# The last norm of a two-layer transformer kernel: squares summed by products with ones, the root from ACT, the row spread into two banks

## The chip, the cores and the metric

The kernel runs on one core of a Trainium2 chip. The metric is the device time of one execution in microseconds (us); lower is better. Engines are named as the profile names them: PE (TensorE), PEld (its weight loads), DVE (VectorE), ACT (ScalarE), POOL (GpSimd), SP (SyncE, here a DMA queue).

## The reference

A hybrid of two layers over 512 positions and 1024 channels, all in float32. Layer 0 mixes with two kinds of attention, layer 1 with a third; each is followed by a convolution-gated FFN with 2816 hidden channels. At the end the whole residual stream goes through one more norm. What matters here is that last norm and the FFN ahead of it:

```python
def rmsnorm(x, g):
    xf = x.astype(jnp.float32)
    y = xf * lax.rsqrt(jnp.mean(xf * xf, axis=-1, keepdims=True) + EPS) * g.astype(jnp.float32)
    return y.astype(x.dtype)

for layer in range(DEPTH):
    h = rmsnorm(x, attn_norm[layer])
    ...
    x = x + conv_glu_ffn(rmsnorm(x, ffn_norm[layer]), w_up[layer], conv_w[layer], conv_b[layer], w_down[layer])
return rmsnorm(x, final_norm)
```

## The kernel before

The residual stream is held transposed: `xT` has eight tiles of 128 channels by 512 positions. Every product of the network is split into three (`mm3`: high by high, high by low, low by high part), which is why PE has almost 6000 matmuls.

In the second layer's FFN, `ffn(1, fin_tile, fin_half, ...)`, the last group of hidden channels is not added over all 512 columns at once but in two halves of 256, `Q[0]` and `Q[1]`. The first half runs over the tiles d = 0 to 7, the second over 6, 7, 4, 5, 2, 3, 0, 1. For each tile PE makes twelve products of 256 columns (`mm_d`, in one of three banks), and DVE adds them to `xT` (L464). Then `fin_tile` is called: ACT squares the tile (`sq`, L776), DVE adds the square to the sum `acc` (L777), and ACT writes tile times gain to an output buffer `yo`, which holds two tiles. After each half `fin_half` is called. It calls `rstd_of`:

- PE transposes `acc` in two blocks of 128 columns into the bank `st_n` (L187), so that positions lie on partitions, and DVE sums each over its 128 elements (L189): `ms_n`, 128x2.
- DVE scales and adds EPS, makes a first guess of the inverse root from the bits of the number (L191, L192), and refines it three times in three steps each (`h`, `h`, `y`; L194 to L196).
- PE transposes `y`, repeated 128 times, back into a bank `bc_n` (L199): each partition then holds the row of inverse roots.

Then ACT copies `bc_n` to `rb` (L786), because POOL cannot read the banks, and eight multiplications follow: six on DVE straight from the bank, those of tiles 3 and 7 on POOL from `rb` (L789). DVE's first one waits until ACT has read the bank. Four DMAs of two tiles each (256 KB) write the half out, two from SP's queue and two from ACT's (L791).

The order of instructions on each engine is set by a scheduler when the program is built, and it interleaves the first half's norm with the second half's products. Up to the last group of the FFN the two programs have the same order on every engine, apart from one memset.

Of the kernel before, what the change touches and what calls it, by code (L numbers as in the profile page):

```python
# [33 lines left out]
EPS = 1e-6  # L34
# [37 lines left out]
def hybrid_kernel(ctx: ExitStack, tc: tile.TileContext, xT_d, pos_d, const_d, vec_d, w_d, out_d, idx):  # L72
    nc = tc.nc
    V, A, G, PE = nc.vector, nc.scalar, nc.gpsimd, nc.tensor

    cp = ctx.enter_context(tc.tile_pool(name="cp", bufs=1))
    wp = ctx.enter_context(tc.tile_pool(name="wp", bufs=3))
    ap_ = ctx.enter_context(tc.tile_pool(name="ap", bufs=1))
# [9 lines left out]
    def tmp(name):  # L88
        return tp.tile([P, T], F32, tag="tmp", name=name, bufs=N_TMP)

    def col(name, n=1):
        return tp.tile([P, n], F32, tag=f"col{n}", name=name, bufs=N_COL)

    def ps(tag, name, shape=(P, T)):
        return pp.tile(list(shape), F32, tag=tag, name=name, bufs=N_PSUM[tag])
# [3 lines left out]
    vec = cp.tile([P, V_END], F32, name="vec")  # L99
    pos = cp.tile([P, NB], I32, name="pos")  # L100
    xT = cp.tile([P, KT, T], F32, name="xT")
# [5 lines left out]
    V.memset(table, 0.0)  # L107
    A.copy(table, table)
    ident = const[:, C_ID:C_ID + P]
    cmask = cp.tile([P, T], F32, name="cmask")  # L110
    G.memset(cmask[:, :384], 0.0)
    selr = cp.tile([P, P + 8], F32R, name="selr")
# [45 lines left out]
    def proj(name, w=None):  # L158
        wh, wl = w or chunk(name)
        o = ps("mm", f"mm_{name}")  # L160
        for k in range(KT):
            s = slice(k * P, k * P + P)
            mm3(o, wh[:, s], wl[:, s], xh[:, k], xl[:, k], k == 0, k == KT - 1)
        return o
# [18 lines left out]
    def rstd_of(acc, n, nm, nb=NB):  # L183

        st = ps("T", f"st_{nm}")[:, :nb * P]
        for b in range(nb):
            PE.transpose(st[:, b * P:b * P + P], acc[:, b * P:b * P + P], ident)  # L187
        ms, y, h, t = (col(f"{c}_{nm}", nb) for c in ("ms", "y", "h", "t"))
        V.reduce_sum(ms, st.rearrange("p (b c) -> p b c", b=nb), axis=mybir.AxisListType.X)  # L189
        V.tensor_scalar(ms, ms, 1.0 / n, EPS, op0=OP.mult, op1=OP.add)  # L190
        V.tensor_scalar(t.bitcast(I32), ms.bitcast(I32), 1, None, op0=OP.logical_shift_right)  # L191
        V.tensor_scalar(y.bitcast(I32), t.bitcast(I32), -1, 0x5F3759DF, op0=OP.mult, op1=OP.add)  # L192
        for _ in range(3):
            V.scalar_tensor_tensor(h, y, -0.5, y, op0=OP.mult, op1=OP.mult)  # L194
            V.tensor_tensor(h, h, ms, op=OP.mult)
            V.scalar_tensor_tensor(y, h, 1.5, y, op0=OP.add, op1=OP.mult)  # L196
        bc = ps("T", f"bc_{nm}")[:, :nb * P]
        for b in range(nb):
            PE.transpose(bc[:, b * P:b * P + P], y[:, b:b + 1].to_broadcast([P, P]), ident)  # L199
        return y, bc  # L200

    scale = {}
# [23 lines left out]
    def scaled(o, nm):  # L226
        y = tmp(f"sc_{nm}")
        V.tensor_tensor(y, o, RB, op=OP.mult)
        return y
# [37 lines left out]
    def rope_angles():  # L267

        def fl(t):
            return t.rearrange("p b f -> p (b f)")  # L270

        def ang_tile(nm, k=1):
            return cp.tile([P, k * NB, 8], F32, name=f"ang_{nm}")

        def rnd(nm, src, k, c=1):
            t = ang_tile(nm, c)
            V.tensor_scalar(fl(t), fl(src), k, MAGIC, op0=OP.mult, op1=OP.add)
            V.tensor_scalar(fl(t), fl(t), -MAGIC, None, op0=OP.add)
# [12 lines left out]
        r, t = ang_tile("r"), ang_tile("t")
        fma(r, hi, -65536.0, ang)
        n0 = rnd("n0", r, 1.0 / TWO_PI)
        n2 = rnd("n2", hi, BIG / TWO_PI)
        V.tensor_scalar(fl(t), fl(hi), M2[0], None, op0=OP.mult)
        for a, k, dst in ((n0, -PI2[0], r), (n2, -PI2[0], t), (n0, -PI2[1], r), (hi, M2[1], t), (n0, -PI2[2], r),
                          (n2, -PI2[1], t), (hi, M2[2], t), (n2, -PI2[2], t)):
            fma(dst, a, k, dst)
        cs = ang_tile("cs", 2)
        V.tensor_tensor(fl(cs[:, NB:]), fl(r), fl(t), op=OP.add)  # L300
        V.tensor_scalar(fl(cs[:, :NB]), fl(cs[:, NB:]), math.pi / 2, None, op0=OP.add)
        k = rnd("k", cs, 1.0 / TWO_PI, 2)
        for p in PI2:
            fma(cs, k, -p, cs)
        V.tensor_scalar(fl(cs), fl(cs), -math.pi, math.pi, op0=OP.max, op1=OP.min)
        A.activation(fl(cs), fl(cs), AF.Sin)
        return cs
# [245 lines left out]
    def sq_acc(n):  # L553
        return cp.tile([P, T], F32, tag="acc", name=f"acc{n}", bufs=1)


    acc = sq_acc(0)
# [6 lines left out]
    cs = rope_angles()  # L564
# [5 lines left out]
    for d in range(KT):  # L570
        if d < 4:
            square(d, acc)
        else:
            s = acc2 if d == 4 else tmp(f"sq{d}")
# [54 lines left out]
    y = scaled(proj("ckv"), "ckv")  # L629
    sq = tmp("sqkv")  # L630
    A.activation(sq, y, AF.Square)
    _, bc = rstd_of(sq, P, "kv")
# [75 lines left out]
    for n in range(8):  # L708
        c, w = (fox if n < 4 else dsa)(n % 4)
# [13 lines left out]
    acc = sq_acc(1)  # L723
# [18 lines left out]
    def moba(p):  # L742
        def vals():
            values["m", p // 2] = v_group(f"mv{p // 2}_", moba_scale if p == 0 else None)

        def qs():
            c["q"] = stack_q(rope(proj(f"mq{p}"), f"mq{p}"), f"mq{p}")

        def ks():
            c["k"] = stack_k(rope(proj(f"mk{p}"), f"mk{p}"), f"mk{p}")  # L750

        c = {"nm": f"m{p}", "v": ("m", p // 2), "hv": 2 * (p % 2), "bias": causal, "out": mo[p // 4]}
        return c, ([vals] if p % 2 == 0 else []) + [ks, qs]

    pairs, work = [], []
    for n in range(8):
        c, w = moba(n)
# [8 lines left out]
    fin = {}  # L766

    def fin_tile(d, cs):
        if cs.start not in fin:
            fin[cs.start] = True  # L770
            fin["acc"] = sq_acc(4 + cs.start)[:, :256]
            fin["y"] = [None] * 4
            A.activation(fin["acc"], xT[:, d, cs], AF.Square)
        else:
            s = tmp(f"sq{d}")[:, :256]
            A.activation(s, xT[:, d, cs], AF.Square)  # L776
            V.tensor_tensor(fin["acc"], fin["acc"], s, op=OP.add)  # L777
        if fin["y"][d // 2] is None:
            fin["y"][d // 2] = ap_.tile([P, 2, 256], F32, tag="big", name=f"yo{cs.start}_{d}", bufs=N_BIG)
        A.activation(fin["y"][d // 2][:, d % 2], xT[:, d, cs], AF.Identity, scale=vec[:, V_G + 32 + d:V_G + 33 + d])  # L780

    def fin_half(cs):
        y = fin["y"]
        _, bc = rstd_of(fin["acc"], D, f"n4_{cs.start}", 2)
        r = tmp(f"rb{cs.start}")[:, :256]
        A.copy(r, bc)  # L786
        for d in range(KT):
            yd = y[d // 2][:, d % 2]
            (G if d % 4 == 3 else V).tensor_tensor(yd, yd, r if d % 4 == 3 else bc, op=OP.mult)  # L789
        for d in range(0, KT, 2):  # L790
            (nc.sync if d % 4 == 0 else nc.scalar).dma_start(out_d[cs.start // 256, :, d:d + 2], y[d // 2])  # L791
# [110 lines left out]
```

## Time and profile before

| | |
|---|---|
| time, median of 3 runs (range) | 1266.65 us (1266.18 to 1268.14) |
| time of the profiled execution | 1267.01 us |
| span of its profile | 1265.2 us |
| mean granted TensorE clock | 0.993 |
| PE busy | 1221.0 us |
| DVE busy | 814.5 us |
| ACT busy | 555.2 us |
| POOL busy | 359.6 us |
| moved by DMA | 127.24 MB |

The span runs from the first to the last instruction of the profiled execution; the time of an execution holds some 1.8 us more. In timeline rows the columns are start, duration, engine, line, operation, output<-inputs, shape and count, and in brackets how long the engine sat idle before and what ended that wait. A DMA row of a queue (SPq, ACTq) is the issue, not the transfer.

### The profile page before, as it was taken

To read this page: it belongs to the slowest core of one execution; us is meant where nothing else is said; L and a number is where in the kernel's file an instruction comes from. 1 tells how busy PE (TensorE), PEld (TensorE's weight loads), DVE (VectorE), ACT (ScalarE), POOL (GpSimd) and SP (SyncE) were. 2 spreads that over 40 slices of the span, in tenths; PEclk is the share of its full clock that TensorE was granted. 3 is DMA by queue.
4 is the path that set the end of the run, shared out by engine and by line. 5 is a ranking of instruction groups with operands and counts; after the bars stand their busy time and mean duration, and the time that the engine had idled before them with its cause. 6 is when DMAs were issued, how large, how long until landed. Compare 5 with 4: busy or idle time off the path is not lost.

```text
span 1265.2 us, 16798 instructions
## 1 busy us (share of the span) xinstructions
PE 1221.0 (97%) x5980; PEld 1017.5 (80%) x5980; DVE 814.5 (64%) x1512; ACT 555.2 (44%) x966; POOL 359.6 (28%) x394
## 2 busy tenths in 40 slices
PE   6889999999999999999998999999999999999996
PEld 4778877777888888888887888888878888888885
DVE  7889988675555445555665778787655555544556
ACT  5564677554333332333434556556433333333234
POOL 3675556542111111111213323232212111111110
PEclk9999999999999999999999999999999999999998
DMA  5344435222333333323334434431323333333321
GB/s 193 101 113 110 114 95 138 68 82 75 94 108 94 98 101 100 95 90 97 103 100 125 112 101 117 108 106 67 97 87 100 100 101 93 92 98 101 100 84 67
DMA packets 57379, 127.24 MB, mean 101 GB/s; under 512 B 7584, under 2 KB 21024, under 8 KB 57296
## 3 DMA queue, kind: packets, MB, share of 16 engines
q1 hardware_dynamic: 56368, 124.81, 33.6%
q10 hardware_dynamic: 864, 1.17, 0.3%
q8 instruction: 47, 0.77, 0.3%
q14 instruction: 36, 0.29, 0.1%
q0 software_dynamic: 64, 0.20, 0.0%
HBM read 104.13 MB, written 2.10 MB: 84 GB/s over the span
## 4 chain that ended last, share of the span: by engine, by line
PE 79%; DVE 12%; ACT 3%; issue 3%; POOL 2%; DMA 2%; DVEq 0%; ACTq 0%; POOLq 0%; SPq 0%
PE mm_d L155 6%; PE mm_d L156 6%; PE mm_d L154 6%; PE mm_u L155 6%; PE mm_u L154 6%; PE mm_u L156 6%; PE mm_g L155 6%; PE mm_g L156 6%; PE mm_g L154 6%; DVE tmask L625 2%; DVE m L624 1%; PE t_m L367 1%; PE o_m L376 1%; PE mm_mk L154 1%; PE mm_mk L155 1%
## 5 line engine op out<-in xcount | busy, mean ns | idle before, releaser
L429 POOL TENSOR_TENSOR cv<-cv,gs 128x512 f32<-128x512 f32 x44 | 57.1, 1298 | 549.7 <-ACT gs L428 549.7
L154 PE MATMUL mm_d<-a_h,wh_d 128*128 128x512 f32 (+1 forms) x384 | 142.9, 372 | 2.2 <-ACT a_h L126 2.2
L155 PE MATMUL mm_d<-a_l,wh_d 128*128 128x512 f32 (+1 forms) x384 | 142.9, 372 | 0.5 <-DVE a_l L127 0.5
L156 PE MATMUL mm_d<-a_h,wl_d 128*128 128x512 f32 (+1 forms) x384 | 142.6, 371 | 0.0
L498 DVE TENSOR_TENSOR us<-mm_u,cv 128x512 f32<-128x512 f32 x44 | 30.4, 691 | 168.2 <-PE mm_u L156 132.7
L155 PE MATMUL mm_g<-xl,wh_g 128*128 128x512 f32 x352 | 137.2, 390 | 0.4 <-DVE xl L170 0.4
L154 PE MATMUL mm_u<-xh,wh_u 128*128 128x512 f32 x352 | 137.3, 390 | 0.0
L156 PE MATMUL mm_u<-xh,wl_u 128*128 128x512 f32 x352 | 137.0, 389 | 0.0
L155 PE MATMUL mm_u<-xl,wh_u 128*128 128x512 f32 x352 | 137.0, 389 | 0.0
L156 PE MATMUL mm_g<-xh,wl_g 128*128 128x512 f32 x352 | 136.9, 389 | 0.0
L154 PE MATMUL mm_g<-xh,wh_g 128*128 128x512 f32 x352 | 136.9, 389 | 0.0
L143 ACT CAST wh_g<-raw_g 128x1024 fp32r<-128x1024 f32 x44 | 46.3, 1053 | 155.4 <-PE mm_g L155 153.9
L495 DVE TENSOR_TENSOR gs<-mm_g,RB 128x512 f32<-128x512 f32 x44 | 30.4, 690 | 121.8 <-PE mm_g L156 119.4
L126 ACT CAST wh_d<-raw_d 128x1024 fp32r<-128x1024 f32 x45 | 47.4, 1054 | 119.3 <-PE mm_u L155 107.3
L154 PEld LDWEIGHTS mm_d<-a_h,wh_d 128*128 128x128 f32 x384 | 72.3, 188 | 15.5 <-ACT a_h L126 3.0
L155 PEld LDWEIGHTS mm_d<-a_l,wh_d 128*128 128x128 f32 x384 | 72.3, 188 | 13.5 <-DVE a_l L127 1.1
L156 PEld LDWEIGHTS mm_d<-a_h,wl_d 128*128 128x128 f32 x384 | 72.3, 188 | 12.4
L155 PEld LDWEIGHTS mm_g<-xl,wh_g 128*128 128x128 f32 x352 | 66.1, 188 | 14.8 <-DVE xl L170 1.1
L154 PEld LDWEIGHTS mm_g<-xh,wh_g 128*128 128x128 f32 x352 | 66.1, 188 | 13.8
L156 PEld LDWEIGHTS mm_u<-xh,wl_u 128*128 128x128 f32 x352 | 66.1, 188 | 13.7
L155 PEld LDWEIGHTS mm_u<-xl,wh_u 128*128 128x128 f32 x352 | 66.1, 188 | 13.6
L154 PEld LDWEIGHTS mm_u<-xh,wh_u 128*128 128x128 f32 x352 | 66.1, 188 | 13.6
(762 smaller groups left out, 3071.9 us busy)
## 6 DMA issues: line engine op xcount, KB each, us to landing
raw_g<-in_w SPq DMA_DIRECT2D x44, 512.0 KB, 3.5
raw_u<-in_w SPq DMA_DIRECT2D x44, 512.0 KB, 3.6
raw_d<-in_w SPq DMA_DIRECT2D x41, 256.0 KB, 2.9
raw_d<-in_w SPq DMA_DIRECT2D x29, 192.0 KB, 2.6
raw_d<-in_w SPq DMA_DIRECT2D x34, 128.0 KB, 2.4
raw_oe<-in_w SPq DMA_DIRECT2D x8, 512.0 KB, 4.2
raw_mv<-in_w SPq DMA_DIRECT2D x8, 512.0 KB, 3.5
raw_mk<-in_w SPq DMA_DIRECT2D x8, 512.0 KB, 4.0
```

The lines of the kernel that those rows point to most:

```text
L126: A.copy(dst_h, src)
L143: A.copy(wh, raw)
L154: PE.matmul(out, ah, bh, start=first, stop=False)
L155: PE.matmul(out, ah, bl, start=False, stop=False)
L156: PE.matmul(out, al, bh, start=False, stop=last)
L367: PE.transpose(t[:, n * P:n * P + P], probs[i][:, j * P:j * P + P], ident)
L376: PE.matmul(o[:, o0:o0 + w], vj, ph[:, c0:c0 + w], start=j == 0, stop=False)
L429: G.tensor_tensor(cv, cv, gs, op=OP.mult)
L495: V.tensor_tensor(gs, og, RB, op=OP.mult)
L498: V.tensor_tensor(us, ou, cv, op=OP.mult)
L624: V.max(m8, sc)
L625: V.match_replace(sc, m8, sc, -3e38)
```

## The change

The helper `rstd_of` stays for the other norms. For the last one `fin_half` now does the work itself:

- The squares are summed over the partitions by products with a tile of ones (`ones`, 128x2, set at the start): the weights are a block of 128 columns of `acc`, and the moving operand is `ones`. The square of the last tile is no longer added to `acc`; it is summed by a product of its own into the same place. Four products per half replace two transposes, the reduction and one addition. Each sum comes out twice, so the column tiles have four columns.
- The inverse root is the reciprocal by DVE, its square root by ACT, and one refinement in three steps.
- The row is spread twice, into `bc` in one bank (read by DVE) and into `bp` in another (read by ACT for POOL's copy).
- DVE multiplies two tiles at a time (three multiplications of 512 elements), and POOL multiplies both tiles of the last pair, 6 and 7.
- Each DMA is issued after its pair, the pairs 0 and 2 from SP, 1 and 3 from ACT. The buffers' names carry the first tile of the pair, so yo_6 is the last pair.

```diff
+    ones = cp.tile([P, 2], F32, name="ones")
+    V.memset(ones, 1.0)
...
     def fin_tile(d, cs):
...
+        f["sq"] = tmp(f"sq{d}")[:, :256] if f["n"] else f["acc"]
+        A.activation(f["sq"], xT[:, d, cs], AF.Square)
+        if 0 < f["n"] < KT - 1:
+            V.tensor_tensor(f["acc"], f["acc"], f["sq"], op=OP.add)
...
     def fin_half(cs):
-        y = fin["y"]
-        _, bc = rstd_of(fin["acc"], D, f"n4_{cs.start}", 2)
+        f = fin[cs.start]
+        nm = f"n4_{cs.start}"
+        st = ps("T", f"st_{nm}")
+        for b in range(2):
+            s = slice(b * P, b * P + P)
+            PE.matmul(st[:, 2 * b:2 * b + 2], f["acc"][:, s], ones, start=True, stop=False)
+            PE.matmul(st[:, 2 * b:2 * b + 2], f["sq"][:, s], ones, start=False, stop=True)
+        ms, y, h = (col(f"{c}_{nm}", 4) for c in ("ms", "y", "h"))
+        V.tensor_scalar(ms, st[:, :4], 1.0 / D, EPS, op0=OP.mult, op1=OP.add)
+        V.reciprocal(h, ms)
+        A.activation(y, h, AF.Sqrt)
+        V.scalar_tensor_tensor(h, y, -0.5, y, op0=OP.mult, op1=OP.mult)
+        V.tensor_tensor(h, h, ms, op=OP.mult)
+        V.scalar_tensor_tensor(y, h, 1.5, y, op0=OP.add, op1=OP.mult)
+        bc, bp = ps("T", f"bc_{nm}")[:, :256], ps("O", f"bp_{nm}")[:, :256]
+        for o in (bc, bp):
+            for b in range(2):
+                PE.transpose(o[:, b * P:b * P + P], y[:, 2 * b:2 * b + 1].to_broadcast([P, P]), ident)
         r = tmp(f"rb{cs.start}")[:, :256]
-        A.copy(r, bc)
-        for d in range(KT):
-            yd = y[d // 2][:, d % 2]
-            (G if d % 4 == 3 else V).tensor_tensor(yd, yd, r if d % 4 == 3 else bc, op=OP.mult)
-        for d in range(0, KT, 2):
-            (nc.sync if d % 4 == 0 else nc.scalar).dma_start(out_d[cs.start // 256, :, d:d + 2], y[d // 2])
+        A.copy(r, bp)
+        for d, yd in sorted(f["y"].items()):
+            if d == 3:
+                for e in range(2):
+                    G.tensor_tensor(yd[:, e], yd[:, e], r, op=OP.mult)
+            else:
+                V.tensor_tensor(yd, yd, bc.rearrange("p (o c) -> p o c", o=1).to_broadcast([P, 2, 256]), op=OP.mult)
+            (nc.sync if d % 2 == 0 else nc.scalar).dma_start(out_d[cs.start // 256, :, 2 * d:2 * d + 2], yd)
```

Line numbers shift by two, and inside `mm3` L154 to L156 become L156 to L158. The numbers in the names below only count tiles; mm_d_6 is the product for tile 6.

PE, before, where the norm of the first half stands among the second half's first products (mm_d_6 and mm_d_7 are the products of tiles 6 and 7, st_n the bank of the transposed sum):

```order
L154 MATMUL mm_d_6_10963<-a_h,wh_d_18_6_10885 128x256
L155 MATMUL mm_d_6_10963<-a_l,wh_d_18_6_10885 128x256
L156 MATMUL mm_d_6_10963<-a_h,wl_d_18_6_10886 128x256
L187 MATMUL st_n_0_10926<-const,acc_10770 128x128 x2
L154 MATMUL mm_d_7_10981<-a_h,wh_d_18_6_10885 128x256
L155 MATMUL mm_d_7_10981<-a_l,wh_d_18_6_10885 128x256
L156 MATMUL mm_d_7_10981<-a_h,wl_d_18_6_10886 128x256
```

After, at the same place, from the last product of the first half's tile 7 on (`ones`, `acc` and `sq` as in the code):

```order
L158 MATMUL mm_d_7_10910<-a_h,wl_d_18_6_10888 128x256
L790 MATMUL st_n_0_10927<-ones,acc_10772 128x2
L156 MATMUL mm_d_6_10958<-a_h,wh_d_18_6_10887 128x256
...
L158 MATMUL mm_d_6_10958<-a_h,wl_d_18_6_10888 128x256
L791 MATMUL st_n_0_10927<-ones,sq_10924 128x2
L790 MATMUL st_n_0_10927<-ones,acc_10772 128x2
L791 MATMUL st_n_0_10927<-ones,sq_10924 128x2
L156 MATMUL mm_d_6_10958<-a_h,wh_d_18_6_10887 128x256
```

One product now stands straight behind the first half's last product; the other three come nine products later, behind the square of tile 7, where before the two transposes came after all twelve products of tile 6.

PE, before, where the row of the first half is spread (bc_n, bp_n its banks; mm_d_2, mm_d_4 and mm_d_5 the products of tiles 2, 4, 5):

```order
L156 MATMUL mm_d_5_11018<-a_h,wl_d_18_4_10842 128x256
L154 MATMUL mm_d_2_11036<-a_h,wh_d_18_2_10796 128x256
L199 MATMUL bc_n_0_10946<-const,y_n_0_10930 128x128 x2
L155 MATMUL mm_d_2_11036<-a_l,wh_d_18_2_10796 128x256
L156 MATMUL mm_d_2_11036<-a_h,wl_d_18_2_10797 128x256
```

After:

```order
L157 MATMUL mm_d_4_10994<-a_l,wh_d_18_4_10843 128x256
L158 MATMUL mm_d_4_10994<-a_h,wl_d_18_4_10844 128x256
L802 MATMUL bc_n_0_10941<-const,y_n_0_10933 128x128 x2
L802 MATMUL bp_n_0_10942<-const,y_n_0_10933 128x128 x2
L156 MATMUL mm_d_4_10994<-a_h,wh_d_18_4_10843 128x256
```

The spreading moved ahead: it stood behind the first product of tile 2, 25 products after the last one of tile 7, and now stands nine products after it, with twice as many transposes.

DVE, before, in the refinement of the first half's root (wl_d is the low part of the last weight buffer, xT with mm_d the addition of a tile):

```order
L195 TENSOR_TENSOR h_n_0_10931<-h_n_0_10931,ms_n_0_10929 128x2
L196 SCALAR_TENSOR_TENSOR y_n_0_10930<-h_n_0_10931,y_n_0_10930 128x2
L127 TENSOR_TENSOR wl_d_18_0_11078<-raw_d_18_0_11073,wh_d_18_0_11077 128x1024
L194 SCALAR_TENSOR_TENSOR h_n_0_10931<-y_n_0_10930 128x2
L464 TENSOR_TENSOR xT<-xT,mm_d_4_10999 128x256
L195 TENSOR_TENSOR h_n_0_10931<-h_n_0_10931,ms_n_0_10929 128x2
L196 SCALAR_TENSOR_TENSOR y_n_0_10930<-h_n_0_10931,y_n_0_10930 128x2
L464 TENSOR_TENSOR xT<-xT,mm_d_5_11018 128x256
L789 TENSOR_TENSOR yo_0_10772<-yo_0_10772,bc_n_0_10946 128x256 x2
L789 TENSOR_TENSOR yo_2_10817<-yo_2_10817,bc_n_0_10946 128x256
```

After, from the first half's ms_n on:

```order
L793 TENSOR_SCALAR ms_n_0_10932<-st_n_0_10927 128x4
L794 RECIPROCAL h_n_0_10934<-ms_n_0_10932 128x4
L466 TENSOR_TENSOR xT<-xT,mm_d_6_10958 128x256
L466 TENSOR_TENSOR xT<-xT,mm_d_7_10976 128x256
L796 SCALAR_TENSOR_TENSOR h_n_0_10934<-y_n_0_10933 128x4
L797 TENSOR_TENSOR h_n_0_10934<-h_n_0_10934,ms_n_0_10932 128x4
L798 SCALAR_TENSOR_TENSOR y_n_0_10933<-h_n_0_10934,y_n_0_10933 128x4
L810 TENSOR_TENSOR yo_0_10774<-yo_0_10774,bc_n_0_10941 128x512
L810 TENSOR_TENSOR yo_2_10819<-yo_2_10819,bc_n_0_10941 128x512
L810 TENSOR_TENSOR yo_4_10864<-yo_4_10864,bc_n_0_10941 128x512
L777 TENSOR_TENSOR acc_10972<-acc_10972,sq_10990 128x256
L466 TENSOR_TENSOR xT<-xT,mm_d_4_10994 128x256
```

The chain is shorter, its step behind ACT's root now stands after the additions of tiles 6 and 7, and the multiplications of yo stand ahead of the addition of tile 4 and of wl_d.

ACT, before, at the very end (squares and yo of tiles 0 and 1, the copy, two output DMAs):

```order
L776 ACTIVATE sq_11095<-xT 128x256
L780 ACTIVATE yo_0_11098<-xT,vec 128x256
L776 ACTIVATE sq_11114<-xT 128x256
L780 ACTIVATE yo_0_11098<-xT,vec 128x256
L786 COPY rb_11141<-bc_n_256_11138 128x256
L791 DMA out<-yo_2_11053 128x512
L791 DMA out<-yo_6_10979 128x512
```

After:

```order
L775 ACTIVATE sq_11090<-xT 128x256
L781 ACTIVATE yo_0_11093<-xT,vec 128x256
L775 ACTIVATE sq_11109<-xT 128x256
L781 ACTIVATE yo_0_11093<-xT,vec 128x256
L795 ACTIVATE y_n_256_11118<-h_n_256_11119 128x4
L804 COPY rb_11132<-bp_n_256_11127 128x256
L811 DMA out<-yo_6_10974 128x512
L811 DMA out<-yo_2_11048 128x512
```

The root stands ahead of the copy, and the two DMAs have changed places: the one of the last pair (yo_6) is first.

More of the change, by code (lines that the diff above doesn't have):

```diff
@@ L768, in fin_tile @@
     def fin_tile(d, cs):
[L769 to L779, printed above, removed]
@@ L780, in fin_tile @@
-        A.activation(fin["y"][d // 2][:, d % 2], xT[:, d, cs], AF.Identity, scale=vec[:, V_G + 32 + d:V_G + 33 + d])
-    def fin_half(cs):
-        y = fin["y"]
-        _, bc = rstd_of(fin["acc"], D, f"n4_{cs.start}", 2)
-        r = tmp(f"rb{cs.start}")[:, :256]
-        A.copy(r, bc)
-        for d in range(KT):
-            yd = y[d // 2][:, d % 2]
-            (G if d % 4 == 3 else V).tensor_tensor(yd, yd, r if d % 4 == 3 else bc, op=OP.mult)
-        for d in range(0, KT, 2):
-            (nc.sync if d % 4 == 0 else nc.scalar).dma_start(out_d[cs.start // 256, :, d:d + 2], y[d // 2])
+        f = fin.setdefault(cs.start, {"n": 0, "y": {}})
@@ new lines, in fin_tile @@
+        if not f["n"]:
+            f["acc"] = sq_acc(4 + cs.start)[:, :256]
+        f["sq"] = tmp(f"sq{d}")[:, :256] if f["n"] else f["acc"]
+        A.activation(f["sq"], xT[:, d, cs], AF.Square)
+        if 0 < f["n"] < KT - 1:
+            V.tensor_tensor(f["acc"], f["acc"], f["sq"], op=OP.add)
+        f["n"] += 1
+        if d // 2 not in f["y"]:
+            f["y"][d // 2] = ap_.tile([P, 2, 256], F32, tag="big", name=f"yo{cs.start}_{d}", bufs=N_BIG)
+        A.activation(f["y"][d // 2][:, d % 2], xT[:, d, cs], AF.Identity, scale=vec[:, V_G + 32 + d:V_G + 33 + d])
```

## The prediction

> **What bounds the kernel now.** I read the page's first part, then the chain of waits, then the timeline of the last 40 us engine by engine, then the busy time of short windows at the very end.
>
> ```profile
> span 1265.2 us, 16798 instructions
> PE 1221.0 (97%) x5980; PEld 1017.5 (80%) x5980; DVE 814.5 (64%) x1512; ACT 555.2 (44%) x966; POOL 359.6 (28%) x394
> ```
>
> PE is busy for 97% of the span, so nothing off PE matters except where PE has run out of work. That is only after the last down product: the chain that ended last leaves PE there and walks through the final norm of the second half of the columns.
>
> ```profile
> 1252.82 0.13 PE mm_d L156
> 1252.98 0.43 DVE xT L464
> 1253.49 0.42 ACT sq L776
> 1253.94 0.43 DVE acc L777
> ...
> 1254.51 0.42 PE st_n L187 x2
> 1254.96 0.43 DVE ms_n L189
> 1255.41 0.18 DVE ms_n L190
> 1255.62 0.18 DVE t_n L191
> ...
> 1257.59 0.17 DVE y_n L196
> 1257.76 0.14 issue
> 1257.90 0.68 PE bc_n L199 x2
> 1258.65 0.38 ACT rb L786
> 1259.06 0.42 DVE yo L789
> ```
>
> From the end of the last square (1253.49 + 0.42 = 1253.91) to the first multiplication of the output (1259.06) it takes 5.15 us, and none of it lies beside PE work. Behind it stands the output.
>
> ```profile
> 1259.06 2.07 DVE L789 TENSOR_TENSOR yo<-yo,bc_n 128x256 f32<-128x256 f32 x6 [1.30 <-ACT rb L786]
> 1259.10 1.41 POOL L789 TENSOR_TENSOR yo<-yo,rb 128x256 f32<-128x256 f32 x2 [9.81 <-ACT rb L786]
> 1259.83 0.33 SPq L791 DMA_DIRECT2D out<-yo  x1
> 1260.22 0.34 ACTq L791 DMA_DIRECT2D out<-yo  x1
> 1261.21 0.34 ACTq L791 DMA_DIRECT2D out<-yo  x1
> 1260.00:1261.00 1.00, 0.00 (x0) 0.00 (x0) 1.00 (x4) 0.00 (x0) 0.51 (x1) 0.50 0.32 121
> 1261.00:1262.00 1.00, 0.00 (x0) 0.00 (x0) 0.13 (x1) 0.00 (x0) 0.00 (x0) 0.50 1.02 385
> 1263.00:1264.00 1.00, 0.00 (x0) 0.00 (x0) 0.00 (x0) 0.00 (x0) 0.00 (x0) 0.50 0.45 168
> ```
>
> In the window rows the last two columns are the DMA share and GB/s. A share of 0.32 in the slice from 1260 means that data began to move near 1260.68, 0.85 after the first issue at 1259.83; from there the engines are full until 1263.45. So the four pieces of 256 KB take 2.77 us together, 0.69 each, and they end 4.39 us after the first multiplication began.
>
> The same norm of the first half lies inside the PE stream, and costs PE only what its own few products and waits cost:
>
> ```profile
> 1239.88 0.43 DVE L777 TENSOR_TENSOR acc<-acc,sq 128x256 f32<-128x256 f32 x1 [0.55 <-ACT sq L776]
> 1240.15 0.28 PE L154 MATMUL mm_d<-a_h,wh_d 128*128 128x256 f32 x1
> 1241.47 0.28 PE L156 MATMUL mm_d<-a_h,wl_d 128*128 128x256 f32 x1
> 1241.89 0.41 PE L187 MATMUL st_n<-const,acc 128*128 128x128 f32 x2
> 1242.26 0.28 PE L155 MATMUL mm_d<-a_l,wh_d 128*128 128x256 f32 x1
> 1246.45 0.28 PE L154 MATMUL mm_d<-a_h,wh_d 128*128 128x256 f32 x1
> 1246.91 0.40 PE L199 MATMUL bc_n<-const,y_n 128*128 128x128 f32 x2 [0.18 <-DVE y_n L196]
> 1247.27 0.28 PE L156 MATMUL mm_d<-a_h,wl_d 128*128 128x256 f32 x1
> ```
>
> A product with 256 columns takes a slot of 0.12 (1240.15 to 1241.47 are eleven of them). Around st_n two slots (0.24) take 0.79, around bc_n 0.82: together 1.13 us of PE time, of which about 0.25 for each pair is the pair itself (the slot at 1241.59 is free, st_n starts at 1241.89, that is 0.30 of waiting) and the rest waiting for DVE.
>
> **The change part by part.** First the prices of operations that the last stage does not have now.
>
> ```profile
> L346 DVE RECIPROCAL sm_m<-sm_m 128x4 f32<-128x4 f32 x16 | 2.8, 173 | 0.9 <-ACT prt_m L344 0.8
> L306 ACT ACTIVATE ang_cs<-ang_cs 128x64 f32<-128x64 f32 x1 | 0.3, 258 | 0.0
> L108 ACT COPY table<-table 128x1 f32<-128x1 f32 x1 | 0.2, 192 | 0.0
> L344 ACT ACT_TABLE_LOAD x2 | 2.6, 1283 | 0.0
> L498 DVE TENSOR_TENSOR us<-mm_u,cv 128x512 f32<-128x512 f32 x44 | 30.4, 691 | 168.2 <-PE mm_u L156 132.7
> 1257.00:1258.00 1.00, 0.10 (x1) 0.14 (x2) 0.65 (x4) 0.00 (x0) 0.00 (x0) 0.74 0.00 0
> 1258.00:1259.00 1.00, 0.56 (x2) 0.16 (x2) 0.00 (x0) 0.35 (x1) 0.00 (x0) 0.50 0.00 0
> ```
>
> *The products with ones* (four per half, weights 128x128, two columns, plain f32) are the unknown. No row shows a plain f32 product that is not a transpose. Call the PE time of one p. From below: the same weights in a transpose cost 0.125 in the stream (the pair's 0.25). From above: the cold pair bc_n, 0.68, for each single product. I take p = 0.3, about the geometric middle, since it is neither a transpose nor an instruction that has nothing beside it. The Trainium skill ("FP8 and Floating Point Precision", TensorE Precision Notes) says that true FP32 takes four passes through the array; no run here shows it yet. By it, with the transpose as one pass, p would be 0.5 and the sum below would end at a loss of 0.7 us.
>
> *First half, in the PE stream.* The first product stands right behind mm_d_7 and waits for the sum with the sixth tile's square, which is ready at 1239.88 + 0.43 + 0.14 (the issue row's hand-over from DVE to PE) = 1240.45, while PE is free at 1240.15: 0.30 lost. Four products: 4p. The row's transposes double, and stand earlier: 9 slots behind mm_d_7's last product instead of 25. DVE's queue puts h and y behind the addition of mm_d_7 to xT, so y cannot be ready before that: product end 0.16 after the slot, hand-over 0.03, h 0.34 after the addition's start (DVE's spacing for 256 columns is 0.33 by the x6 row: (2.07 - 0.42) / 5), then two steps of 0.2 and 0.16, hand-over 0.14, in all 1.24 us, against 9 slots = 1.08. PE waits 0.16 and spends 4 x 0.125 = 0.5. Sum 0.30 + 4p + 0.66, against 1.13 before: PE's last product moves later by 4p - 0.17, which is 1.03 us. The first half's table load (1.283 us from about 1241.6, when ACT is through with the last yo tile) is over near 1242.9, before DVE turns to h near 1245, so it costs nothing; without that cover h would start up to 1.3 later, and PE with it. ACT now holds its two output DMAs ahead of the squares of tile 4, and they wait for POOL (its multiplication starts near 1247 and takes 1.41); ACT then has six squares and six yo tiles left, about 0.75 a pair, 4.5 in all, while PE still has some 45 slots, 5.4 us, so the squares are back on time for the last tile. DVE's three wide multiplications stand ahead of the additions of tiles 4 and 5, whose banks PE needs only about 2 us later. The memset of ones (DVE, at the start) lies in DVE's wait for the first input. All of these: nothing.
>
> *Second half, on the path.* The addition of the last square (0.43 with its start 0.03) goes, its place being taken by a product. From the end of the square: hand-over to PE 0.14 (taken as DVE's), then three products, since the one on the older sum is already done: two spacings of p and a last one's length of 0.28. Then ms 0.03 + 0.21, reciprocal 0.17, hand-over 0.09 (1253.41 to 1253.49), root 0.21 (between the COPY's 0.19 and the 0.26 of 64 columns), 0.03, three steps 0.20 + 0.20 + 0.17, 0.14, transposes 0.68, 0.04 to DVE, which no longer waits for ACT's copy. Without the products 2.31; with them 2.59 + 2p = 3.19 instead of 5.15. Gain 1.96. The reduction (0.43), shift and guess, six of nine refinement steps and the wait for rb (0.41) are what is in it.
>
> *The output.* The first pair is done 0.69 after the start instead of 0.75; the third at 0.69 + 0.60 + 0.60 = 1.89. But POOL now has both tiles of the last pair, and starts later: bp's transposes come behind bc's (about 0.55 more while cold), then the copy 0.07 + 0.38, 0.04, and POOL's 1.41, so it is ready 2.40 after DVE's start. ACT's queue has that pair's DMA ahead of the second pair's, which has been ready since 1.29: issues at about 0.71 and 1.91 (SP), 2.48 and 2.9 (ACT). With 0.85 to the first byte and 0.69 each the last byte falls at 4.85, against 4.39. Loss 0.46.
>
> Sum: -1.03 + 1.96 - 0.46 = 0.47, rounded to a gain of 0.4 us; in p it is 2.27 - 6p. The profiled execution took 1267.01, which is its span and 1.8 around it, 0.36 above the median of 1266.65; I take the difference from the median: 1266.2. With p at 0.125 the gain is 1.5, and 2.0 to 2.3 if the transposes also run warm. The clock in the rows above falls to half within 1257 to 1258, so bc_n is cold (0.68 against 0.40 in the stream); after the change it would start near 1257.4, on that edge. The Trainium skill ("TensorE: Matmul & The Clock Gate", Part 1) says that the gate acts at the ends of a free-running window of 3.4 us, by which either can happen from run to run; the sum has it cold. With p at 0.68 the loss is 1.8.
>
> About 0.2%, 2.5 us, is what a measurement of this kernel can tell from no change; gain and loss stay inside it.
>
> **The rivals.**
> 1. *Products dear enough to turn it slower.* If one product costs four times a full product length without overlap, 4 x 0.28 = 1.1, PE loses 4.2 in the first half and the path gains only 0.4: 2.27 - 6.6 = -4.3, 1271.0 us. It decides from p = 0.8 on (2.27 - 4.8 = -2.5). For it: nothing in the trace prices this form. Against: in the stream weight loads overlap (80% PEld busy beside 97% PE).
> 2. *Four passes at a transpose's price*, p = 0.5: 1267.4 us, the first half's loss (1.8) eating the end's gain. This is the sentence of the Trainium skill above taken as a forecast.
> 3. *Everything cheap*: p = 0.125 and warm transposes, and the output not delayed because the copy from bp starts early: 2.3 and a little more, 1264.2 us. Against: ACT's order of the two DMAs is fixed.
> 4. *A shift elsewhere.* Ones stands ahead of the weight buffers, and moves all tiles allotted later by 32 bytes. One ns on each of 5980 products would be 6 us either way. Nothing in the rows shows that addresses matter: mm_g's xh and mm_d's a_h lie in different pools, and both run at the same spacing.
>
> **How the numbers follow.** My sum with p from 0.13 to 0.4: 0.52. Rival 2: 0.24. Rival 3: 0.12, a third of it beyond 0.2%. Rival 1: 0.07, nearly all beyond. Rival 4: 0.05, split. Faster 0.04 + 0.02 = 0.06, slower 0.07 + 0.02 = 0.09, same 0.85. The range reaches to p = 0.68 (1268.4) and to rival 3's edge (1264.5).
>
> **What would show it.** Right: the last down product of PE about 1 us later than 1252.66; first multiplication near 1258.1; POOL's pair as the last to be ready, and a dip in the DMA share between the first and the second piece; one more table load, beside PE work. Wrong: products with ones that show as several instructions each or over 0.5 us apart (rival 2 or 1); a PE wait for y far above 0.16; a spacing of mm_g other than before (rival 4).

## The result, and the profile after

| | before | after |
|---|---|---|
| time, median (range), 6 runs each | 1267.63 us (1266.18 to 1269.61) | 1282.05 us (1276.91 to 1282.41) |
| span of the profiled execution | 1265.2 us | 1280.3 us |
| granted TensorE clock | 0.993 | 0.993 |

The ratio is 1.0103, with an interval of 1.0083 to 1.0122: the changed kernel is slower by about 1%, 14 us, where the prediction had a gain of 0.4 us and a range up to 1268.4. The first lines of the page after:

```profile
span 1280.3 us, 16801 instructions
PE 1240.3 (97%) x5996; PEld 1018.8 (80%) x5996; DVE 812.4 (63%) x1489; ACT 557.8 (44%) x969; POOL 359.9 (28%) x394
```

PE has 16 instructions more and is busy for 19.3 us more, with the same share of the span. So the kernel does not wait more; PE's products themselves take longer. Where, is read from the starts of the same products in both timelines. First the kernel before (first gate product of layer 0, its last, the same two of layer 1, and the first product of 256 columns, which is where the changed part begins):

```profile
273.15 0.39 PE L154 MATMUL mm_g<-xh,wh_g 128*128 128x512 f32 x1
...
611.48 0.39 PE L156 MATMUL mm_u<-xh,wl_u 128*128 128x512 f32 x1
...
887.95 0.39 PE L154 MATMUL mm_g<-xh,wh_g 128*128 128x512 f32 x1
...
1225.69 0.39 PE L156 MATMUL mm_u<-xh,wl_u 128*128 128x512 f32 x1
...
1228.64 0.28 PE L154 MATMUL mm_d<-a_h,wh_d 128*128 128x256 f32 x1
```

The same products after:

```profile
275.99 0.40 PE L156 MATMUL mm_g<-xh,wh_g 128*128 128x512 f32 x1
...
621.54 0.40 PE L158 MATMUL mm_u<-xh,wl_u 128*128 128x512 f32 x1
...
896.83 0.40 PE L156 MATMUL mm_g<-xh,wh_g 128*128 128x512 f32 x1
...
1241.87 0.40 PE L158 MATMUL mm_u<-xh,wl_u 128*128 128x512 f32 x1
...
1244.85 0.28 PE L156 MATMUL mm_d<-a_h,wh_d 128*128 128x256 f32 x1
```

The changed part begins 16.21 us later than before. The stretch up to layer 0's FFN lost 2.84, the two FFNs 7.22 and 7.30, layer 1's mixing gained 1.18. All of that code is unchanged. The figures of the FFNs can be relied on: in the traces of before and of all runs below whose gate and up products run at the spacing of before, the same stretches take 338.33 to 338.38 and 337.75 to 337.81. The other two can't: in those traces the first product of layer 0's FFN starts anywhere from 273.15 to 277.21, and layer 1's mixing takes 272.47 to 276.47, so one trace of each kernel doesn't show what the change costs there. From the first product of 256 columns to the end of the span it takes 36.56 before (1265.2 - 1228.64) and 35.45 after (1280.3 - 1244.85): **the edited part is 1.11 us faster, and the loss lies wholly ahead of it.** In what follows "the tail" is this stretch.

Within an FFN, two rows of the timeline before, 21 gate products apart:

```profile
483.87 0.39 PE L154 MATMUL mm_g<-xh,wh_g 128*128 128x512 f32 x1
...
488.63 0.39 PE L154 MATMUL mm_g<-xh,wh_g 128*128 128x512 f32 x1
```

and two rows after, 23 products apart:

```profile
482.63 0.40 PE L156 MATMUL mm_u<-xh,wh_u 128*128 128x512 f32 x1
...
487.99 0.40 PE L158 MATMUL mm_u<-xh,wl_u 128*128 128x512 f32 x1
```

4.76 / 21 = 0.2267 us before, 5.36 / 23 = 0.2330 after. On 1056 such products in each FFN that is some 6.7 us of the 7.2 to 7.3; the down products take the rest (their spacing went from 0.2267 to 0.2288 on average: of each twelve the first six spacings are 0.228 to 0.236, the other six 0.227 as before). Nothing in the order of these instructions changed. What changed is where their operands lie: `ones` is padded to 32 bytes on each partition, and the weight buffers (wh, wl), which are allotted behind it, moved by 32 bytes, and so did the tiles behind them, a_h and a_l among them, while xh and xl, ahead of it, did not. In the layout of the program before, the pool of the weight buffers begins 61,952 bytes behind xh, 121 times 512; after, 61,984. The distance from that pool to the one of a_h stays at 36,864 bytes, 72 times 512. (The single buffers and the blocks in them follow each other in steps of 512 bytes or multiples, so every pair of weights and moving data has the same distance modulo 512.)

Now the tail, the timeline after (first half's sums and spread, then the second half's end):

```profile
1256.24 0.28 PE L158 MATMUL mm_d<-a_h,wl_d 128*128 128x256 f32 x1
1256.66 0.35 PE L790 MATMUL st_n<-ones,acc 128*128 128x2 f32 x2
...
1261.46 0.28 PE L158 MATMUL mm_d<-a_h,wl_d 128*128 128x256 f32 x1
1261.74 0.40 PE L802 MATMUL bc_n<-const,y_n 128*128 128x128 f32 x2
...
1269.62 0.28 PE L158 MATMUL mm_d<-a_h,wl_d 128*128 128x256 f32 x1
1270.53 0.42 ACT L775 ACTIVATE sq<-xT 128x256 f32<-128x256 f32 x1 [0.48 <-DVE xT L466]
1271.00 0.38 PE L791 MATMUL st_n<-ones,sq 128*128 128x2 f32 x2 [0.39 <-ACT sq L775]
1271.24 0.36 PE L790 MATMUL st_n<-ones,acc 128*128 128x2 f32 x2
1271.47 0.36 PE L791 MATMUL st_n<-ones,sq 128*128 128x2 f32 x2
1273.22 0.66 PE L802 MATMUL bc_n<-const,y_n 128*128 128x128 f32 x2 [1.39 <-DVE y_n L798]
1273.91 1.88 DVE L810 TENSOR_TENSOR yo<-yo,bc_n 128x512 f32<-128x512 f32 x3 [0.84 <-PE bc_n L802]
1274.84 1.41 POOL L808 TENSOR_TENSOR yo<-yo,rb 128x256 f32<-128x256 f32 x2 [10.46 <-ACT rb L804]
1276.29 0.85 ACTq L811 DMA_DIRECT2D out<-yo  x2
```

Each product with ones is two instructions (x2) and takes 0.235 us (1271.00, 1271.24, 1271.47). And the windows of the output after; the last two columns are the DMA share and GB/s:

```profile
1275.00:1276.00 1.00, 0.00 (x0) 0.00 (x0) 0.79 (x2) 0.00 (x0) 1.00 (x2) 0.50 0.50 188
1276.00:1277.00 1.00, 0.00 (x0) 0.00 (x0) 0.00 (x0) 0.00 (x0) 0.25 (x1) 0.50 0.55 203
1277.00:1278.00 1.00, 0.00 (x0) 0.00 (x0) 0.00 (x0) 0.00 (x0) 0.00 (x0) 0.50 1.02 381
1278.00:1279.00 1.00, 0.00 (x0) 0.00 (x0) 0.00 (x0) 0.00 (x0) 0.00 (x0) 0.50 0.78 277
```

The share dips to 0.55 between the first and the later pieces; the last byte lands near 1278.78.

### The profile page after: what moved, and what is told of

Its sections match the earlier page's. It is cut to its first block, busy times and chain, and to the rows that moved or that the text cites. A ratio compares the mean times of both kernels' runs of the same rounds, so it can differ in the third digit from the quotient of the medians.

```text
span 1280.3 us, 16801 instructions
## 1 busy us (share of the span) xinstructions
PE 1240.3 (97%) x5996; PEld 1018.8 (80%) x5996; DVE 812.4 (63%) x1489; ACT 557.8 (44%) x969; POOL 359.9 (28%) x394
## 5 line engine op out<-in xcount | busy, mean ns | idle before, releaser
L156 PE MATMUL mm_d<-a_h,wh_d 128*128 128x512 f32 (+1 forms) x384 | 143.8, 374 | 1.2 <-ACT a_h L128 1.2
L158 PE MATMUL mm_d<-a_h,wl_d 128*128 128x512 f32 (+1 forms) x384 | 142.6, 371 | 0.0
L156 PE MATMUL mm_u<-xh,wh_u 128*128 128x512 f32 x352 | 139.6, 397 | 0.0
L156 PE MATMUL mm_g<-xh,wh_g 128*128 128x512 f32 x352 | 139.3, 396 | 0.0
L158 PE MATMUL mm_g<-xh,wl_g 128*128 128x512 f32 x352 | 139.2, 396 | 0.0
L158 PE MATMUL mm_u<-xh,wl_u 128*128 128x512 f32 x352 | 139.2, 395 | 0.0
L156 PEld LDWEIGHTS mm_d<-a_h,wh_d 128*128 128x128 f32 x384 | 72.3, 188 | 16.0 <-ACT a_h L128 2.1
L158 PEld LDWEIGHTS mm_d<-a_h,wl_d 128*128 128x128 f32 x384 | 72.4, 188 | 13.1
L158 PEld LDWEIGHTS mm_u<-xh,wl_u 128*128 128x128 f32 x352 | 66.1, 188 | 16.0
L158 PEld LDWEIGHTS mm_g<-xh,wl_g 128*128 128x128 f32 x352 | 66.1, 188 | 16.0
L156 PEld LDWEIGHTS mm_g<-xh,wh_g 128*128 128x128 f32 x352 | 66.1, 188 | 15.8
L156 PEld LDWEIGHTS mm_u<-xh,wh_u 128*128 128x128 f32 x352 | 66.1, 188 | 15.6
```

Of the source, the lines that this page charges most:

```text
L156: PE.matmul(out, ah, bh, start=first, stop=False)
L158: PE.matmul(out, al, bh, start=False, stop=last)
```

## The experiments

**Is it the shift?** Theory R says that the distance in memory between the weights and the moving data of a product counts, W that the weights' own address does, N that the addresses have nothing to do with it. The first kernel is the one before with the tile alone; nothing uses it.

```diff
+    ones = cp.tile([P, 2], F32, name="ones")
+    V.memset(ones, 1.0)
```

> The kernel before with nothing but the tile of ones and its memset, so that xh and xl stay and all later tiles, the weight buffers first, lie 32 bytes higher. Theory R (a product is slower when its weights and its moving data lie 32 bytes apart modulo 64): mm_g and mm_u every 0.233 us instead of 0.227, and 1282 to 1284 us. Theory W (the weights' own address, 0 modulo 64, is what is slow): the same, 1283. Rival N (addresses don't matter; the new last norm itself, its table load or its products slow PE down): nothing of the norm is in this kernel, so 1267 us and 0.227.

Measured: 1283.6 us (1281.15 to 1285.18), ratio 1.0117 (1.0092 to 1.0142), gate and up products 0.2334 apart; the tail takes 36.62, as in the kernel before. An unused tile of 32 bytes makes the whole loss. N falls.

The changed kernel with `ones` padded to 64 bytes:

```diff
-    ones = cp.tile([P, 2], F32, name="ones")
+    ones = cp.tile([P, 16], F32, name="ones")[:, :2]
```

> The changed kernel with ones allotted 16 columns, 64 bytes, of which two are used: all later tiles move by 64 instead of 32. R and W: mm_g and mm_u back at 0.227, and the whole at 1266 us, about 1 us below the kernel before, since from the first half-width product to the end the changed kernel took 35.45 us and the one before 36.56. Rival N: unchanged, 1282 us.

Measured: 1279.36 us (1276.78 to 1281.83), ratio 1.0088 (1.0065 to 1.011), spacing 0.2333. This was missed: whatever counts, it does not count modulo 64.

The changed kernel with `ones` allotted as the first tile of its pool, so that xh, xl, the weights and all else move together:

```diff
+    ones = cp.tile([P, 2], F32, name="ones")
...
-    ones = cp.tile([P, 2], F32, name="ones")
     V.memset(ones, 1.0)
```

> The changed kernel with ones allotted ahead of all other tiles: xT, xh and xl move by 32 bytes too, and every distance between moving data and weights is as it was, but all addresses are 0 modulo 64 where they were 32. R: 0.227 and 1266 us. W (the weights' own address counts): still 0.233 and 1282 us. Rival N: 1282 us.

Measured: 1266.4 us (1262.68 to 1267.19), ratio 0.999 (0.9976 to 1.0004), spacing 0.2267 for all three kinds of product, tail 35.27. All addresses are other than before, the distances are the same, and the loss is gone. W falls.

The kernel before with a gap of 32 bytes behind the weight buffers, so that a_h and a_l move against the weights and xh and xl don't:

```diff
+    wp.tile([P, 8], F32, tag="gap", bufs=1, name="gap")
```

> The kernel before with an unused tile of 32 bytes behind the weight buffers: xh, xl and the weights stay at 32 modulo 64, while the FFN's a_h and a_l and the attention's o_h, o_l move to 0. R: mm_g and mm_u at 0.227, but mm_d and the output projections at 0.233; 960 + 192 products of 512 columns by 6.6 ns are 7.6 us, so 1273 to 1275 us. W: all at 0.227, 1267 us. Rival N: 1267 us.

Measured: 1274.4 us (1274.04 to 1276.74), ratio 1.0053 (1.0034 to 1.0072). Two rows of the groups before (mean ns stands ahead of the last bar):

```profile
L154 PE MATMUL mm_u<-xh,wh_u 128*128 128x512 f32 x352 | 137.3, 390 | 0.0
...
L154 PE MATMUL mm_d<-a_h,wh_d 128*128 128x512 f32 x320 | 124.7, 390 | 2.2 <-ACT a_h L126 2.2
```

and the same two with the gap:

```profile
L154 PE MATMUL mm_u<-xh,wh_u 128*128 128x512 f32 x352 | 138.2, 393 | 0.0
...
L154 PE MATMUL mm_d<-a_h,wh_d 128*128 128x512 f32 x320 | 127.1, 397 | 2.1 <-ACT a_h L126 2.1
```

Now it is the down products that are slow (0.234 apart), and the gate and up products only follow them by a little (0.228: the first eight or so behind each group of down products take 0.226 to 0.239, the later ones 0.227). The loss moves with the pair of operands whose distance changed. So the distance is what counts, shown in both directions: with all addresses moved and the distances kept the loss is gone, and with one distance alone changed it comes back for the products of that distance. Modulo what, is still open here.

One thing goes the other way. The products of 256 columns in this run's tail, whose distance changed too, run 0.1173 apart instead of 0.1199, and PE needs 23.64 from the first of them to the last instead of 24.02. With that and with transposes that ran warm (at full granted clock, 0.26 us less) its tail takes 35.94 (1272.6 - 1236.66) where the same code took 36.56.

**Which distances?** A program of its own, run once: 28 settings of 36 products, with fixed moving data and the weights starting at a chosen distance `o`. The core of its loop:

```diff
...
+    for i in range(36):
+        w = o // 4 + P * ((i // 2) % 8)
+        PE.matmul(acc[:, :n], W[:, w:w + P], X[:, i % KT, :n], start=i == 0, stop=i == 35)
...
```

> No part of the network: 36 products in a row for each of 28 settings, weights from one tile in steps of 512 bytes, moving data from another, the distance between the two modulo 512 set to 0, 32, ... 480 bytes, again 0, then 4, 8, 16, 48 (512 columns), and 0, 16, 32, 64, 128, 256, 384 (256 columns). Theory R, as it stands after the shift of 64 was as slow as the one of 32: 0.227 us per product at distance 0 and 0.233 at every other. A variant, the modulus is 128 or 256: 0.227 comes back at 128 or 256. Rival D (not the distance inside one product but something of the whole program, such as which buffer other engines write at the time): the same spacing at all settings, since no other engine runs beside these products.

Seven rows of its timeline: 32, 192, 256 and 0 bytes modulo 512, then 16, all with 512 columns; then 256 columns at 0 and at 64:

```profile
25.35 8.67 PE L96 MATMUL acc<-X,W 128*128 128x512 f32 x36 [0.78 <-DVE y L97]
...
72.60 8.52 PE L96 MATMUL acc<-X,W 128*128 128x512 f32 x36 [0.78 <-DVE y L97]
...
91.35 8.46 PE L96 MATMUL acc<-X,W 128*128 128x512 f32 x36 [0.78 <-DVE y L97]
...
166.58 8.46 PE L96 MATMUL acc<-X,W 128*128 128x512 f32 x36 [0.78 <-DVE y L97]
...
194.61 8.44 PE L96 MATMUL acc<-X,W 128*128 128x512 f32 x36 [0.78 <-DVE y L97]
...
213.27 4.57 PE L96 MATMUL acc<-X,W 128*128 128x256 f32 x36 [0.78 <-DVE y L97]
...
228.44 4.36 PE L96 MATMUL acc<-X,W 128*128 128x256 f32 x36 [0.52 <-DVE y L97]
```

With 512 columns 0, 256 and 16 are fast; 192 and 448 took 8.52, 8 took 8.59, and all others 8.63 to 8.70 (0 is read from its repetition, as the very first setting ran with a cold PE). The difference of 0.21 over some 35 spacings is 6 ns, the size seen in the network. It repeats after 256 bytes: theory R with "0.233 at every other" was wrong about 256, its variant with the modulus 256 fits, and rival D falls. At 512 columns no distance ran clearly faster than the one that the kernel before had by the way its tiles happened to fall.

With 256 columns the distance counts too, but the other way round: 4.57 at 0 and at 256, 4.52 to 4.54 at 16, 32, 128 and 384, and 4.36 at 64. That fits the tail of the kernel with the gap, whose products of 256 columns ran faster at 32 than at 0.

The second series, again one run, asks for finer steps and for other kinds of product. Its edit is the list of settings; the bf16 copies take the same loop.

```diff
+    runs = [("r", o, T) for o in (0, 0, 16, 20, 24, 28, 32, 48, 112, 144, 176, 208, 224, 240, 248, 252)]
+    runs += [("same", o, T) for o in (0, 32)]
+    runs += [("b", o, T) for o in (0, 32, 64, 128, 256, 384)]
+    runs += [("r", o, 384) for o in (0, 32)]
```

> No part of the network: 26 settings of 36 products each, one after the other, as in the series before (there 36 products took 8.46 us at distances 0 and 256, 8.44 at 16, 8.52 at 192 and 448, 8.59 to 8.70 at all others; these are the profile's spans of 36). The distance is that of the weights' start from the moving data's, modulo 256 bytes. Settings in order: fp32r, 512 columns at 0 (cold), 0, 16, 20, 24, 28, 32, 48, 112, 144, 176, 208, 224, 240, 248, 252; the same weights 36 times at 0 and 32; bf16 at 0, 32, 64, 128, 256, 384; fp32r with 384 columns at 0 and 32. Theory C (the load of the next weights reads beside the moving data, and the two collide when their starts stand wrongly): differences at every kind, the same weights too; fast at 0 and 16 and, by symmetry, at 240. Rival K (a matter of 4-byte data alone): bf16 equal within 0.05 us at all six. Rival A (only multiples of 16 in a window of 0 to 16 are fast): 8.65 at 20, 24, 28, 240, 248 and 252. Rival S (it hangs on the weights changing): the same weights take equal times at 0 and 32.

Six rows of its timeline: fp32r at 0, at 16 and at 240; the same weights at 0; bf16 at 32; 384 columns at 32:

```profile
25.00 8.48 PE L109 MATMUL acc<-X,W 128*128 128x512 f32 x36 [0.78 <-DVE y L110]
34.27 8.66 PE L109 MATMUL acc<-X,W 128*128 128x512 f32 x36 [0.79 <-DVE y L110]
...
137.98 8.46 PE L109 MATMUL acc<-X,W 128*128 128x512 f32 x36 [0.78 <-DVE y L110]
...
166.13 8.46 PE L109 MATMUL acc<-X,W 128*128 128x512 f32 x36 [0.78 <-DVE y L110]
...
193.54 7.93 PE L106 MATMUL acc<-Xb,Wb 128*128 128x512 bf16 x36 [0.78 <-DVE y L110]
...
244.29 6.54 PE L109 MATMUL acc<-X,W 128*128 128x384 f32 x36 [0.65 <-DVE y L110]
```

The other settings of fp32r with 512 columns took 8.55 to 8.69. The same weights 36 times took 8.46 at 0 and 8.67 at 32: it does not hang on the weights changing, and rival S falls. bf16 took 7.93 at all six distances, as rival K has it, and theory C falls as far as it said "every kind". But 4-byte data alone are not the whole of it either, since 384 columns of fp32r took 6.54 at both distances tried. Rival A falls at 240.

One thing stays open: the distance 16 took 8.44 in the first series and 8.66 in this one, with the same operands. The starts within the settings say a little more. At 0 and 256 the spacings behind the first are slow for five to nine products (mostly 0.228 to 0.236) and then settle at 0.227; the down products after do the same, six slow and then fast, in every group of twelve. At 16 they settled after two in the first series and never in the second; at 192 they go on between 0.225 and 0.236, 0.229 in the mean. What decides whether the products settle, and what in PE or memory the distance acts on, was not shown.

The second check in the network is the changed kernel with `ones` padded to 256 bytes.

```diff
-    ones = cp.tile([P, 2], F32, name="ones")
+    ones = cp.tile([P, 64], F32, name="ones")[:, :2]
```

> The changed kernel at its own place in the code, with ones padded to 256 bytes, so that the weight buffers and all later tiles stand 256 bytes further than before instead of 32 (the tile of 64 bytes took 1279.4). Theory M (the distance between weights and moving data counts modulo 256, as in the first series, where 36 products took 8.46 us at 0 and at 256): mm_g, mm_u and mm_d at 226.7 ns, 1264.5 to 1267, the first product of 256 columns to the end of the span 35.2 to 35.6. Rival L (only the very distance of the kernel before is fast in the network, or modulo more than 256): mm_g and mm_u at 233, 1279 to 1284.

Measured: 1266.7 us (1262.56 to 1270.7), ratio 0.9997 (0.9983 to 1.0012), all three kinds of product 0.2267 to 0.2268 apart, tail 35.44. The row of its groups is the one before again, 390 ns:

```profile
L156 PE MATMUL mm_u<-xh,wh_u 128*128 128x512 f32 x352 | 137.3, 390 | 0.0
```

Same code, the same order on PE, the same tile at the same place: 32 bytes cost 14 us, 64 bytes 12, 256 bytes nothing. Theory M holds.

**What is the edit itself worth?** Three kernels on top of the one with `ones` first. The root done the old way:

```diff
-        V.reciprocal(h, ms)
-        A.activation(y, h, AF.Sqrt)
+        V.tensor_scalar(h.bitcast(I32), ms.bitcast(I32), 1, None, op0=OP.logical_shift_right)
+        V.tensor_scalar(y.bitcast(I32), h.bitcast(I32), -1, 0x5F3759DF, op0=OP.mult, op1=OP.add)
+        for _ in range(3):
...
```

> The kernel with ones allotted first, with one part undone: the inverse root is again a guess from the bits and three refinements on DVE, over four columns. Theory (the terms of the sum, each operation at its own duration): from the end of the last square to the first multiplication 2.70 (there with warm transposes) becomes 2.70 - 0.20 (reciprocal) - 0.45 (root from ACT and both hand-overs) + 8 x 0.19 = 3.6 to 3.8, and 3.9 to 4.1 if the transposes fall cold by being later; PE's wait in the first half changes by under 0.2, so 35.27 becomes 36.2 to 36.6. Rival (ACT's root costs as much as it saves, since its hand-overs stand on the path): 35.2 to 35.4.

Measured in a single run: 1266.41 us, tail 36.81. From the end of the square (1253.89) to the first multiplication it takes 4.17:

```profile
1258.06 1.88 DVE L811 TENSOR_TENSOR yo<-yo,bc_n 128x512 f32<-128x512 f32 x3 [0.91 <-PE bc_n L803]
```

The transposes were cold here (the granted clock had fallen to half, and they took 0.66), as in the changed kernel, so the 4.17 stand against its 2.96: the root is worth 1.21, a little more than expected. In the kernel with `ones` first they were warm:

```profile
1253.99 0.40 PE L802 MATMUL bc_n<-const,y_n 128*128 128x128 f32 x2 [1.39 <-DVE y_n L798]
...
1254.43 1.88 DVE L810 TENSOR_TENSOR yo<-yo,bc_n 128x512 f32<-128x512 f32 x3 [0.59 <-PE bc_n L802]
```

That is 2.70 from the end of its square at 1251.73, 0.26 less than cold. The code of the tail doesn't decide it: the same tail ran warm in the kernel with 64 bytes too, and cold in the one with 256. The old spread:

```diff
-        for o in (bc, bp):
...
-        A.copy(r, bp)
+        A.copy(r, bc)
+        for d in range(KT):
+            yd = f["y"][d // 2][:, d % 2]
+            (G if d % 4 == 3 else V).tensor_tensor(yd, yd, r if d % 4 == 3 else bc, op=OP.mult)
```

> The kernel with ones allotted first, with the other part undone: one bank bc, copied by ACT for POOL before DVE reads it, six multiplications of one tile on DVE and two on POOL, as before. Theory (the spread brings 0.4 on the path and loses 0.25 to 0.45 in the output): square's end to first multiplication 2.70 becomes 3.1, output from there 6.47 becomes 6.1, together 35.2 to 35.4, no difference. Rival S (the spread is the greater part of the gain): 36.0 or more. Rival L (the spread loses, since POOL's pair is late): 34.9 or less.

Measured in a single run: 1264.84 us, tail 35.83, cold transposes. The square ends at 1253.38, and

```profile
1256.81 2.08 DVE L806 TENSOR_TENSOR yo<-yo,bc_n 128x256 f32<-128x256 f32 x6 [1.30 <-ACT rb L803]
```

that is 3.43 against 2.96, and 6.29 from there to the end against 6.39. So the spread brings 0.47 on the path and loses some 0.1 in the output (the spans are given to 0.1), 0.3 to 0.4 together, between the theory and rival S; rival L falls. And the last pair sent from SP:

```diff
-            (nc.sync if d % 2 == 0 else nc.scalar).dma_start(...)
+            (nc.sync if d in (0, 3) else nc.scalar).dma_start(...)
```

> The kernel with ones allotted first (time 1266.4, first product of 256 columns to the end of the span 35.27 us), with one edit: the last pair of the output (tiles 6 and 7, POOL's) goes out from SP's queue behind pair 0, and pair 2 from ACT's behind pair 1. Theory O (the output is held by ACT's order, in which pair 1, ready since 0.6 us, waits for POOL): the DMA share no longer dips between the first and the second piece, the last byte comes 0.3 us earlier, 35.27 becomes 34.9 to 35.0. Rival T (the engines' 2.77 us for 1 MB and the start of the first piece set the end): 35.2 to 35.3, no dip and no gain. By both the whole time is 1264.5 to 1266.5, 1.3 to 1.7 us of profile below the kernel before, which the rounds can hardly tell from none.

Measured: 1264.98 us (1262.75 to 1267.55), ratio 0.9991 (0.998 to 1.0001); tail 35.03, with cold transposes.

```profile
1256.21 1.88 DVE L810 TENSOR_TENSOR yo<-yo,bc_n 128x512 f32<-128x512 f32 x3 [0.84 <-PE bc_n L802]
...
1258.00:1259.00 1.00, 0.00 (x0) 0.00 (x0) 0.10 (x1) 0.00 (x0) 0.55 (x1) 0.50 1.04 387
1259.00:1260.00 1.00, 0.00 (x0) 0.00 (x0) 0.00 (x0) 0.00 (x0) 0.00 (x0) 0.50 1.02 369
```

The dip is gone, and the output takes 5.99 (1262.2 - 1256.21) against 6.39: theory O holds, at 0.40. This is the lowest median of the kernels that ran several times. Its tail is 1.5 us shorter than the tail before, but a ratio with this interval can't be told from no change.

## Why the prediction was wrong

**The step that failed is the one that dismissed rival 4.** The sum took every product ahead of the tail to run as before, a term put at nothing. Rival 4 named the place (`ones` stands ahead of the weight buffers and moves all later tiles by 32 bytes) and dismissed it, with a chance of 0.05 and a price of 1 ns on each product. Its reason was that mm_g's xh and mm_d's a_h lie in different pools and both run at the same spacing. The rows were read rightly and prove nothing: both distances were multiples of 512 bytes before (121 and 72 times), so the trace of before held two samples of one and the same case. The price was 6.3 to 6.7 ns on the 2112 gate and up products and 2 ns on the down products, 14.5 us in the two FFNs. The projections of the mixing that read xh slowed too (layer 1's mm_mq from 0.2281 to 0.2331 apart), but what that costs in all can't be read from traces that differ by more there. The sign named there as showing it, "a spacing of mm_g other than before", is the one that appeared. The range had no room for it.

The Trainium skill ("TensorE: Matmul & The Clock Gate", Part 2: What happens when you issue a matmul) says that TensorE reads SBUF through two independent ports, one for the streamed operand and one for the weights, and that products in a row follow each other at one column per cycle. For bf16 the runs here agree: 36 products took 7.93 us at each of the six distances tried, some 0.216 apart. For fp32r at 512 columns they don't: 8.46 or 8.67 by the distance between the two operands. That it is the two reads that hinder each other would fit this, but no run shows it.

**The other terms** came out within 0.3 us each, three of the four better than predicted. They sum to the 1.11 that the tail gained, against 0.47 predicted. Both traces here had cold transposes; among all runs the tail's code of before took 36.56 and 36.62, and 35.94 with the gap, and the changed one 35.22 to 35.45. So the gain is there in each pair, but its size is that of two single traces.

| term | predicted | measured |
|---|---|---|
| PE's last product, first half's norm in its stream | -1.03 | -0.75 (24.02 to 24.77 from the first product of 256 columns) |
| last product to the square's end | 0 | -0.08 (1.25 to 1.33) |
| square's end to first multiplication | +1.96 | +2.19 (5.15 to 2.96) |
| output | -0.46 | -0.25 (6.14 to 6.39) |

- *Products with ones.* p was taken at 0.3 and is 0.235. With it the formula of the first half, 4p - 0.17, gives 0.77 against 0.75. Its two waits were right: 0.30 ahead of st_n (1256.24 + 0.12 to 1256.66) and 0.16 ahead of bc_n (1261.46 + 0.12 to 1261.74). So rivals 1 and 2, with p at 0.8 and 0.5, fall, though one of their signs appeared: each product shows as two instructions. The Trainium skill ("FP8 and Floating Point Precision", TensorE Precision Notes) speaks of four passes for true FP32; the trace shows two load and product pairs for each product with ones, and at two columns they cost less than half of what four transposes would (0.235 against 4 x 0.125). Whether each pair makes two of the four passes, no run shows.
- *Second half.* 2.59 + 2p is 3.06 with the measured p; it took 2.96, mostly because the products start 0.05 behind the square (1270.53 + 0.42 to 1271.00) and not 0.14. By the runs, 1.21 of the 2.19 is the root and 0.47 the spread; the remaining 0.51 falls to the sums, by difference alone. The transposes were cold in the changed kernel (0.66), as the sum had them, and warm in two other runs of the same tail (0.40), so the edge was as close as the prediction said.
- *Output.* POOL's pair was the last, ready 2.34 after DVE's start (2.40 predicted), the dip is there, and the last byte fell 4.87 after the start (4.85 predicted). Only what follows the last byte was shorter, 1.5 us against 1.75, so that 0.25 was lost instead of 0.46.
- *Rival 3* had the tail at 2 us and more; with p near a quarter and cold transposes it got half of that.

With the shift taken out, the times are 1266.4 and 1266.7, where the kernel before, measured beside them, took 1266.48 and 1267.37. That lies in the predicted range and close to the predicted 1266.2, but times can't tell a gain of 0.4 from one of 1.1 or from none: the terms above rest on the traces.

## What to carry to other kernels

A new tile, however small and whatever it is for, moves every tile allotted behind it: before and after an edit compare the distances between weights and moving data, and where fp32r products of 512 columns bound the kernel, keep them at a multiple of 256 bytes. With 256 columns, time it: there a multiple of 256 was the slowest of the distances tried, with 512 the fastest. Allot small tiles first in their pool, or pad them to 256 bytes, and read the spacing of an unchanged product in both traces before looking for the loss in the edit. Two operands that run alike say nothing about an address unless their addresses differ in the way that is asked about.

## What the runs showed of the hardware

- fp32r products of 512 columns run 0.2267 us apart when weights and moving data lie a multiple of 256 bytes apart, and 0.233 to 0.234 at most other distances tried.
- At 256 columns fp32r products depend on the distance the other way: 36 of them took 4.57 us at 0 and at 256 bytes, 4.36 at 64, and 4.52 to 4.54 at the others tried; in the network they ran 0.1199 apart at 0 and 0.1173 at 32.
- bf16 of 512 columns (36 in 7.93 us, six distances) and fp32r of 384 columns (6.54, two distances) show no difference.
- Slow products can settle into the fast spacing after some six, as at 0 and 256 bytes, and at 16 bytes they did in one series (8.44) and not in the other (8.66). What decides it was not found.
- A plain f32 product with two columns is two load and product pairs, together 0.235 us in a row of three such products.
